# Decay-level products in blocks of 32, and state products of two chunks at once, in a two-layer hybrid trunk

## The chip, the cores and the metric

The kernel runs on one core of a Trainium2 chip. The metric is device time in microseconds (us), from the first to the last instruction with what lies around them; the smaller the better. The engines are PE (TensorE, matmuls), DVE (VectorE), ACT (ScalarE), POOL (GpSimd) and SP (which issues most DMAs). Each runs its own queue in order and waits for others by semaphores.

## The reference, cut to what matters

Two layers work on 512 latent tokens and 128 context tokens of width 1024. In each layer one projection feeds three groups of heads whose outputs meet in one output projection, followed by a feed-forward block. The change touches one of the three, a bidirectional gated recurrence (HGRN2, 6 heads of 64), and the last step that it shares with the retention heads:

```python
def body(S, inp):                       # _hgrn2_chunked, one direction
    qc, bc, kc, vc = inp                # bc: running sum of log forget gates
    inter = jnp.einsum('bhid,bhdv->bhiv', qc * jnp.exp(bc), S)
    rel = bc[:, :, :, None, :] - bc[:, :, None, :, :]
    dec = jnp.exp(jnp.where(tri[:, :, None], rel, -jnp.inf))
    A = jnp.sum(qc[:, :, :, None, :] * kc[:, :, None, :, :] * dec, axis=-1)
    o = inter + jnp.einsum('bhij,bhjv->bhiv', A, vc)
```

It runs once forward and once on the flipped sequence, and the two outputs are added. Retention (`_retention_chunked`) has the same shape with one decay number per head.

## The kernel before

Heads go in pairs: a *channel tile* `ct` (0, 1, 2) holds two heads, head `hh` on partitions 64·hh to 64·hh+63. The 512 latent tokens are four chunks `u` of 128. A fourth call with `ct` None takes the 128 context tokens of all three pairs, as three "chunks".

`hgrn(l, ct)` builds the 128 x 128 matrix A of each chunk and head, both directions at once, transposed (keys on partitions), in the tile `AT`. The decay between key and query depends on the channel, so it cannot be applied after one product. Instead there are eight products: a diagonal one (PSUM tiles `pd`) and one for each of seven *levels* 0 to 6 (`pl`). Level `lev` holds the pairs whose positions lie in the two halves of one aligned block of 2·2^lev tokens. Before each level the queries `Qx` have been multiplied by forget products of the level below (line 855, on DVE), the keys `K` likewise on POOL, and ACT has laid the keys out again as `C` (`composite`). Each product is cut into blocks: in the kernel before, 64 keys by 64 queries, so a chunk and head has two blocks and a call has 4 chunks x 2 heads x 2 blocks = 16 matmuls per product (12 for context). The contraction is over the 64 channels of a head, the result goes to partitions 64·b of the PSUM tile of its head. What a level's 64 x 64 block holds beyond that level is masked off: levels 0 to 4 go into `AT` by a predicated copy on DVE (line 860, mask `msk`), level 5 by eight ACT copies of 32 partitions (line 865), level 6, whose pairs lie in different blocks of 64, by four ACT copies (line 869), after one ACT copy (line 857) has moved the second block's part of `AT` to its place.

`cross_out` makes the output of one `ct` in the PSUM tile `o`. For each chunk: two directions x two heads of state times decayed queries (line 741: 64 channels by 64 outputs by 128 tokens, partitions of head `hh` in and out), then two products with `AT` (line 745: 128 keys). One ACT copy (line 757) takes all four chunks to `raw`. `retention` calls it too. The feed-forward and the projections use matmuls of a type with one pass (`mm3`, lines 220 to 222: three products of high and low parts); all of the above are plain float32.

PE's order is fixed by the program: `Order` steps threads (`hgrn`, `retention`, `fourier` and so on) by a clock of its own, advanced by `o.pe(...)`, and a level is issued 2.4 of those microseconds after the one before it at the earliest, with projection matmuls between. The order on the other engines is made by a list scheduler from its own estimates. PSUM is eight banks handed out in turn.

Names on DVE in the rows below: `jb` is a product-and-sum of the modulation (lines 313 and 315), `wlo` the low part of a weight tile (line 208), `rx` and `rxs` the rotary step of retention, `F`, `PF`, `K`, `PK` the gates.

Of the kernel before, what the change touches and what calls it, by code (L numbers as in the profile page):

```python
# [11 lines left out]
U8 = mybir.dt.uint8  # L12
# [17 lines left out]
def pick(t2, p0, p1, off, dims):  # L30
    b = t2[p0:p1, 0:1]
    return bass.AP(b.tensor, b.offset + off, [list(list(b.ap)[0])] + [list(d) for d in dims])
# [119 lines left out]
class Kernel:  # L152
# [313 lines left out]
    def mixers(self, l, hT, mp):  # L466
        nc, a, o = self.nc, self.a, self.o
# [6 lines left out]
        self.raws, self.mix = [None] * 6, [None] * NK  # L474
        mskf = self.m4("mskf", (128, 7, 128))
        nc.sync.dma_start(mskf, a["masks"])
        self.msk = mp.tile([128, 5, 64], U8, name="msk")
        for b in (slice(0, 64), slice(64, 128)):
            nc.vector.tensor_copy(self.msk[b], mskf[b, 0:5, b])
        self.free(mskf)  # L480
        self.forget_bounds(l)
        self.PF, self.PK = self.m3("PF", (128, 2, 3, 128)), self.m3("PK", (128, 2, 3, 128))
# [246 lines left out]
    def cross_out(self, kind, ct, AT, S, Qd, V):  # L729
        nc = self.nc  # L730
        base = 3 if kind == 0 else 0
        po = self.ps("o")
        nu = 3 if ct is None else 4
        for u in range(nu):
            tt, cc = (4, u) if ct is None else (u, ct)
            out = po[:, u * 128:(u + 1) * 128]
            if ct is not None:
                for d in range(2):
                    for hh in range(2):
                        hs = slice(64 * hh, 64 * hh + 64)  # L740
                        nc.tensor.matmul(out[hs], S[hs, d, u if d == 0 else 3 - u, :], Qd[d][hs, u * 128:(u + 1) * 128],
                                         start=(d == 0), stop=False)
            for hh in range(2):
                v = V[cc][:, tt] if ct is not None or kind else self.prompt_v(cc)[:, 0]
                nc.tensor.matmul(out[64 * hh:64 * hh + 64], v[:, 64 * hh:64 * hh + 64], AT[:, hh, u, :],
                                 start=(ct is None), stop=True)
        self.o.pe(3.2 if ct is not None else 1.0)
        self.free(AT)
        if ct is None:
            for c in range(3):  # L750
                nc.scalar.copy(self.raws[base + c][:, 512:640], po[:, c * 128:(c + 1) * 128])
            self.free(*V)
        else:
            self.free(S)
            self.owed -= kind == 0
            self.raws[base + ct] = self.get("ax", "raw", (128, T))
            nc.scalar.copy(self.raws[base + ct][:, 0:512], po)

    def center(self, out, x, n, heads=2):

# [9 lines left out]
    def hgrn(self, l, ct):  # L770
# [3 lines left out]
        nc = self.nc  # L774
# [4 lines left out]
        if ct is None:  # L779
            bases = (self.PF, self.PK, self.Pq)  # L780
            F, K = (t.rearrange("p d c w -> p d (c w)") for t in (self.PF, self.PK))
            q = self.Pq.rearrange("p c w -> p (c w)")
        else:
            bases = self.hg.pop(ct)
            F, K, q = bases
        nu = 3 if ct is None else 4
        W = nu * 128
        Qx = self.m4("Qx", (128, 2, W))
        ks = self.m2("ks", (128, W))
        nc.gpsimd.tensor_tensor(ks, K[:, 0, :], K[:, 1, :], ALU.add)  # L790
        nc.vector.tensor_tensor(Qx, F, q.unsqueeze(1).to_broadcast([128, 2, W]), ALU.mult)
        AT = self.m4("AT", (128, 2, nu, 128))
        Qf, Kf = Qx.rearrange("p d w -> p (d w)"), K.rearrange("p d w -> p (d w)")
# [5 lines left out]
        def composite(lev):  # L799
            s = 1 << lev  # L800
            C = self.mem.again(Cs.popleft(), "C", (128, W))
            Cs.append(C)
            nc.scalar.copy(pick(C, 0, 128, 0, [[2 * s, W // s // 2], [s, 2], [1, s]]),
                           pick(Kf, 0, 128, 0, [[2 * s, W // s // 2], [W + s, 2], [1, s]]))
            return C

        C = composite(0)
# [2 lines left out]

        A = AT.rearrange("p h u i -> p (h u) i")

        def halves(name):
            return [self.ps(name)[:, 0:W // 2].rearrange("p (u i) -> p u i", u=nu) for _ in range(2)]

        def blocks():
            for u in range(nu):
                for hh in range(2):
                    for b in range(2):
                        t0 = u * 128 + 64 * b  # L820
                        yield slice(64 * hh, 64 * hh + 64), slice(64 * b, 64 * b + 64), hh, u, b, t0

        pd = halves("pd")
        for pr, rows, hh, u, b, t0 in blocks():
            nc.tensor.matmul(pd[hh][rows, u], ks[pr, t0:t0 + 64], q[pr, t0:t0 + 64], start=True, stop=True)
        self.o.pe(0.44 * nu)
        self.free(ks, bases[2])
        for hh in range(2):
            nc.scalar.copy(AT[:, hh, :, 0:64], pd[hh])
        yield 1.0  # L830
        S = None
        for lev in range(7):
            s = 1 << lev
            nb = W // s
            np_ = nb // 2
            pl = halves("pl")
            for pr, rows, hh, u, b, t0 in blocks():
                if lev < 6:
                    qs = pick(Qf, pr.start, pr.stop, t0, [[2 * s, 32 // s], [W + s, 2], [1, s]])
                else:  # L840
                    qs = Qf[pr, (1 - b) * W + t0 + 64 - 128 * b:(1 - b) * W + t0 + 128 - 128 * b]
                nc.tensor.matmul(pl[hh][rows, u], C[pr, t0:t0 + 64], qs, start=True, stop=True)
            self.o.pe(0.44 * nu)

            for d in range(2):
                kv = pick(Kf, 0, 128, d * (W + s), [[2 * s, np_], [1, s]])
                tv = pick(Tt, 0, 128, toff + (nb + 1 if d == 0 else 0), [[2, np_], [0, s]])
                self.kv.tensor_tensor(kv, kv, tv, ALU.mult)
            if lev < 6:
                C = composite(lev + 1)  # L850
            self.kv.tensor_tensor(pick(Tn, 0, 128, tnext, [[np_, 2], [1, np_]]),
                                  pick(Tt, 0, 128, toff, [[nb, 2], [2, np_]]),
                                  pick(Tt, 0, 128, toff + 1, [[nb, 2], [2, np_]]), ALU.mult)
            qv = pick(Qf, 0, 128, 0, [[W + s, 2], [2 * s, np_], [1, s]])
            nc.vector.tensor_tensor(qv, qv, pick(Tt, 0, 128, toff + 1, [[nb - 1, 2], [2, np_], [0, s]]), ALU.mult)
            if lev == 6:
                nc.scalar.copy(A[64:128, :, 64:128], A[64:128, :, 0:64])
            for hh in range(2):
                if lev < 5:
                    nc.vector.copy_predicated(AT[:, hh, :, 0:64], self.msk[:, lev, :].unsqueeze(1).to_broadcast([128, nu, 64]),  # L860
                                              pl[hh])
                elif lev == 5:
                    for b in range(4):
                        rows, cols = slice(32 * b, 32 * b + 32), slice(32 - 32 * (b % 2), 64 - 32 * (b % 2))
                        nc.scalar.copy(AT[rows, hh, :, cols], pl[hh][rows, :, cols])
                else:
                    for b in range(2):
                        rows = slice(64 * b, 64 * b + 64)
                        nc.scalar.copy(AT[rows, hh, :, 64 - 64 * b:128 - 64 * b], pl[hh][rows])
            Tt, toff, tnext = Tn, tnext, tnext + 2 * np_  # L870
            if lev == 0:
                self.free(bases[0])
            if lev == 5:
                self.free(*Cs)
            if lev == 4 and ct is not None:
                yield lambda: self.can(m4=1)
                S = self.new_states(l, 1, ct)
            if lev == 1:
                self.mark(("Hfree", ct))
            yield P["lev"]  # L880
# [4 lines left out]
        for d in range(2):  # L885
            for n in range(3):
                u = n if ct is None or d == 0 else n + 1
# [634 lines left out]
```

## Time and profile before

| | |
|---|---|
| Median of three runs | 1721.58 us (1717.36 to 1722.53) |
| Profiled execution | 1719.44 us |
| its span, first to last instruction | 1717.7 us |
| around the span | 1.7 us |
| PE busy | 1651.0 us, 96% |
| DVE busy | 1056.3 us, 61% |
| ACT busy | 698.5 us, 41% |
| POOL busy | 452.5 us, 26% |

The stage with the changed functions ("mixers") lasts from about 97 to 320 us in layer 0 and from about 940 to 1145 us in layer 1; the rest is projections and feed-forward. Busy time of PE counts overlapping matmuls once.

### The profile page before, as it was taken

To read this page: it belongs to the slowest core of one execution; us is meant where nothing else is said; L and a number is where in the kernel's file an instruction comes from. 1 tells how busy PE (TensorE), PEld (TensorE's weight loads), DVE (VectorE), ACT (ScalarE), POOL (GpSimd) and SP (SyncE) were. 2 spreads that over 40 slices of the span, in tenths; PEclk is the share of its full clock that TensorE was granted. 3 is DMA by queue.
4 is the path that set the end of the run, shared out by engine and by line. 5 is a ranking of instruction groups with operands and counts; after the bars stand their busy time and mean duration, and the time that the engine had idled before them with its cause. 6 is when DMAs were issued, how large, how long until landed. Compare 5 with 4: busy or idle time off the path is not lost. (4 is left out here: it accounts for less than half of the span.)

```text
span 1717.7 us, 31084 instructions
## 1 busy us (share of the span) xinstructions
PE 1651.0 (96%) x12594; PEld 1517.4 (88%) x12594; DVE 1056.3 (61%) x1849; ACT 698.5 (41%) x1368; POOL 452.5 (26%) x474
## 2 busy tenths in 40 slices
PE   6989898999999999999999999999999999999997
PEld 4888787888999998989989988879799999999996
DVE  4788966458668776777493547664754434343428
ACT  4534443826544443434164444485352222121210
POOL 2134532104355453544042334320310000000002
PEclk9999999999999999999999999999999999999999
DMA  9544411243355454544123122024134222121201
GB/s 343 189 136 151 132 52 39 68 176 109 121 194 185 160 181 139 184 135 155 66 102 104 63 77 70 31 72 162 47 114 144 76 73 87 62 92 56 99 25 62
DMA packets 70991, 194.55 MB, mean 113 GB/s; under 512 B 11952, under 2 KB 12736, under 8 KB 70848
## 3 DMA queue, kind: packets, MB, share of 16 engines
q1 hardware_dynamic: 66528, 182.10, 31.7%
q0 software_dynamic: 4032, 10.35, 1.7%
q8 instruction: 99, 1.62, 0.4%
q14 instruction: 44, 0.36, 0.1%
q10 hardware_dynamic: 288, 0.11, 0.0%
HBM read 186.47 MB, written 6.06 MB: 112 GB/s over the span
## 5 line engine op out<-in xcount | busy, mean ns | idle before, releaser
L208 DVE TENSOR_TENSOR wlo<-wraw,whi 128x1024 fp32r<-128x1024 f32 x204 | 268.3, 1316 | 242.9 <-ACT whi L207 237.2
L207 ACT CAST whi<-wraw 128x1024 fp32r<-128x1024 f32 x206 | 214.9, 1048 | 400.0 <-PE pg L221 128.0
L317 POOL TENSOR_TENSOR wm<-wm,csb 128x512 f32<-128x512 f32 x112 | 178.9, 1616 | 184.3 <-DVE jb L313 171.1
L222 PE MATMUL pg<-h2T,wlo 128*128 128x384 f32 (+1 forms) x704 | 218.2, 310 | 3.2 <-DVE wlo L208 3.1
L220 PE MATMUL pg<-h2T,whi 128*128 128x384 f32 (+1 forms) x704 | 218.3, 310 | 0.0
L221 PE MATMUL pg<-h2T,whi 128*128 128x384 f32 (+1 forms) x704 | 217.8, 309 | 0.0
L221 PE MATMUL pu<-h2T,whi 128*128 128x384 f32 (+1 forms) x704 | 217.2, 308 | 0.0
L222 PE MATMUL pu<-h2T,wlo 128*128 128x384 f32 (+1 forms) x704 | 217.2, 308 | 0.0
L220 PE MATMUL pu<-h2T,whi 128*128 128x384 f32 (+1 forms) x704 | 217.2, 308 | 0.0
L341 POOL TENSOR_SCALAR bnve<-bnag 128x1 f32<-128x1 f32 x40 | 13.8, 350 | 657.2 <-DVE bnag L339 652.6
L220 PE MATMUL dps<-whi,ah 128*128 128x512 f32 x440 | 171.6, 390 | 0.0
L222 PE MATMUL dps<-whi,al 128*128 128x512 f32 x440 | 171.5, 390 | 0.0
L221 PE MATMUL dps<-wlo,ah 128*128 128x512 f32 x440 | 171.4, 389 | 0.0
L313 DVE SCALAR_TENSOR_TENSOR jb<-wm,csb 128x512 bf16<-128x512 f32 x160 | 149.0, 931 | 16.7 <-DMA wm<-in_w_modT 10.8
L222 PEld LDWEIGHTS pg<-h2T,wlo 128*128 128x128 f32 x704 | 134.0, 190 | 3.7 <-DVE wlo L208 3.6
L290 ACT ACTIVATE wm<-wm 128x512 f32<-128x512 f32 x112 | 70.8, 632 | 158.5 <-POOL wm L317 158.3
L220 PEld LDWEIGHTS pg<-h2T,whi 128*128 128x128 f32 x704 | 134.2, 191 | 0.3
L221 PEld LDWEIGHTS pg<-h2T,whi 128*128 128x128 f32 x704 | 134.1, 191 | 0.3
L221 PEld LDWEIGHTS pu<-h2T,whi 128*128 128x128 f32 x704 | 133.7, 190 | 0.0
L220 PEld LDWEIGHTS pu<-h2T,whi 128*128 128x128 f32 x704 | 133.7, 190 | 0.0
L222 PEld LDWEIGHTS pu<-h2T,wlo 128*128 128x128 f32 x704 | 133.6, 190 | 0.0
L1216 DVE TENSOR_TENSOR sg<-sg,pu 128x256 f32<-128x256 f32 x88 | 42.7, 485 | 119.6 <-PE pu L222 113.0
(277 smaller groups left out, 3752.9 us busy)
## 6 DMA issues: line engine op xcount, KB each, us to landing
wm<-in_w_modT SPq DMA_DIRECT2D x160, 256.0 KB, 2.9
wraw<-in_w_gate SPq DMA_DIRECT2D x44, 512.0 KB, 3.8
wraw<-in_w_up SPq DMA_DIRECT2D x44, 512.0 KB, 3.4
wraw<-in_w_down SPq DMA_DIRECT2D x44, 512.0 KB, 3.3
wraw<-in_w_fm SPq DMA_DIRECT2D x42, 512.0 KB, 3.3
wm<-in_w_mod SPq DMA_DIRECT2D x16, 512.0 KB, 10.2
wraw<-in_w_tm SPq DMA_DIRECT2D x16, 512.0 KB, 3.4
wraw<-in_w_out SPq DMA_DIRECT2D x16, 512.0 KB, 3.3
```

The costliest lines, as they stand in the source:

```text
L207: self.nc.scalar.copy(hi, raw)
L208: (eng or self.nc.vector).tensor_tensor(lo, raw, hi.bitcast(F32), ALU.subtract)
L220: mm(out, lh, rh, start=first, stop=False)
L221: mm(out, lh, rl, start=False, stop=False)
L222: mm(out, ll, rh, start=False, stop=last)
L290: keep(nc.scalar.activation(out=t, in_=t, func=AF.Copy, accum_out=d))
L313: keep(nc.vector.scalar_tensor_tensor(self.jb, wt, 1.0, csb[0], ALU.mult, ALU.mult, accum_out=d[0]))
L317: nc.gpsimd.tensor_tensor(wt, wt, csb[1], ALU.mult)
L341: nc.gpsimd.tensor_scalar(ve, ag[:, 1:2], EPS, None, ALU.add)
L1216: nc.vector.tensor_tensor(sg, sg, pu[:, :n], ALU.mult)
```

## The change

All products but level 6 are now made of blocks of 32 keys by 32 queries: a chunk and head has four of them, and a product 32 matmuls (24 for context) that go to partitions 32·b. PSUM, the ACT copy of the diagonal, the mask and the predicated copies are half as wide. Level 5 is no longer inside a block: its queries come from the neighbouring block of 32, and its eight ACT copies put it beside the diagonal blocks. The blocks that belong on the diagonal of `AT` are moved there by three ACT copies at level 5 (one copy at level 6 before). `cross_out` has two PSUM tiles and takes two chunks together; the second chunk's heads write to swapped halves of the second tile, so four state products in a row use four different pairs of input and output halves. The second tile leaves PSUM by two ACT copies that cross partitions, the first by one.

```diff
-        self.msk = mp.tile([128, 5, 64], U8, name="msk")
+        self.msk = mp.tile([128, 5, 32], U8, name="msk")
...
-        po = self.ps("o")
...
+        po = [self.ps("o") for _ in range(1 if ct is None else 2)]
+        for a in range(0, 3 if ct is None else 4, len(po)):
+            dst = [(u, hh, po[x][64 * (hh ^ x):64 * (hh ^ x) + 64, (u // len(po)) * 128:(u // len(po)) * 128 + 128])
+                   for x, u in enumerate(range(a, a + len(po))) for hh in range(2)]
             if ct is not None:
                 for d in range(2):
-                    for hh in range(2):
+                    for u, hh, out in dst:
                         hs = slice(64 * hh, 64 * hh + 64)
-                        nc.tensor.matmul(out[hs], S[hs, d, u if d == 0 else 3 - u, :], Qd[d][hs, u * 128:(u + 1) * 128],
+                        nc.tensor.matmul(out, S[hs, d, u if d == 0 else 3 - u, :], Qd[d][hs, u * 128:(u + 1) * 128],
...
-            nc.scalar.copy(self.raws[base + ct][:, 0:512], po)
+            raw = self.raws[base + ct][:, 0:512].rearrange("p (a x i) -> p x a i", a=2, x=2)
+            ov = [p[:, 0:256].rearrange("p (a i) -> p a i", a=2) for p in po]
+            nc.scalar.copy(raw[:, 0], ov[0])
+            for hh in range(2):
+                nc.scalar.copy(raw[64 * hh:64 * hh + 64, 1], ov[1][64 - 64 * hh:128 - 64 * hh])
...
-        pd = halves("pd")
-        for pr, rows, hh, u, b, t0 in blocks():
-            nc.tensor.matmul(pd[hh][rows, u], ks[pr, t0:t0 + 64], q[pr, t0:t0 + 64], start=True, stop=True)
+        pd = parts("pd", 32)
+        for pr, rows, hh, u, b, t0 in blocks(32):
+            nc.tensor.matmul(pd[hh][rows, u], ks[pr, t0:t0 + 32], q[pr, t0:t0 + 32], start=True, stop=True)
...
+            n = max(s, 32)
+            pl = parts("pl", n)
+            for pr, rows, hh, u, b, t0 in blocks(n):
+                if lev < 5:
+                    qs = pick(Qf, pr.start, pr.stop, t0, [[2 * s, 16 // s], [W + s, 2], [1, s]])
                 else:
-                    qs = Qf[pr, (1 - b) * W + t0 + 64 - 128 * b:(1 - b) * W + t0 + 128 - 128 * b]
-                nc.tensor.matmul(pl[hh][rows, u], C[pr, t0:t0 + 64], qs, start=True, stop=True)
+                    i0 = (1 - b % 2) * W + t0 + n - 2 * n * (b % 2)
+                    qs = Qf[pr, i0:i0 + n]
+                nc.tensor.matmul(pl[hh][rows, u], C[pr, t0:t0 + n], qs, start=True, stop=True)
...
-            if lev == 6:
-                nc.scalar.copy(A[64:128, :, 64:128], A[64:128, :, 0:64])
+            if lev == 5:
+                for b in range(1, 4):
+                    rows = slice(32 * b, 32 * b + 32)
+                    nc.scalar.copy(A[rows, :, rows], A[rows, :, 0:32])
...
-                    nc.vector.copy_predicated(AT[:, hh, :, 0:64], self.msk[:, lev, :].unsqueeze(1).to_broadcast([128, nu, 64]),
+                    nc.vector.copy_predicated(AT[:, hh, :, 0:32], self.msk[:, lev, :].unsqueeze(1).to_broadcast([128, nu, 32]),
```

On PE the groups of matmuls stand in the same sequence as before; only their number changes. Here is the end of the first channel tile in layer 0, where `cross_out` is followed by the diagonal product of the second tile, on PE, before:

```order
L741 MATMUL o<-Qx,S 64x128 x4
L745 MATMUL o<-AT,VH_135 64x128 x2
L741 MATMUL o<-Qx,S 64x128 x4
L745 MATMUL o<-AT,VH_135 64x128 x2
L741 MATMUL o<-Qx,S 64x128 x4
L745 MATMUL o<-AT,VH_135 64x128 x2
L741 MATMUL o<-Qx,S 64x128 x4
L745 MATMUL o<-AT,VH_135 64x128 x2
L825 MATMUL pd<-q,ks 64x64 x16
```

and of the changed kernel:

```order
L742 MATMUL o<-Qx,S 64x128 x8
L747 MATMUL o<-AT,VH_135 64x128 x4
L742 MATMUL o<-Qx,S 64x128 x8
L747 MATMUL o<-AT,VH_135 64x128 x4
L829 MATMUL pd<-q,ks 32x32 x32
```

Eight turns between the two kinds of product have become four, and the 16 matmuls of the diagonal 32.

On DVE the scheduler has moved other work. In layer 0, first channel tile, around the query product that ends level 3 (`Qx`, 128x2x32x8), before:

```order
L313 SCALAR_TENSOR_TENSOR jb,acc<-wm,csb 128x512
L208 TENSOR_TENSOR wlo<-wraw,whi 128x1024
L315 SCALAR_TENSOR_TENSOR jb,acc<-wm,csb 128x512
L855 TENSOR_TENSOR Qx<-Qx,Tm 128x2x32x8
L860 COPY_PREDICATED AT<-msk,pl 128x4x64 x2
```

and of the changed kernel, where the query product has line 861 and the predicated copy line 868:

```order
L313 SCALAR_TENSOR_TENSOR jb,acc<-wm,csb 128x512
L315 SCALAR_TENSOR_TENSOR jb,acc<-wm,csb 128x512
L861 TENSOR_TENSOR Qx<-Qx,Tm 128x2x32x8
L868 COPY_PREDICATED AT<-msk,pl 128x4x32 x2
L313 SCALAR_TENSOR_TENSOR jb,acc<-wm,csb 128x512
L208 TENSOR_TENSOR wlo<-wraw,whi 128x1024
```

The low part of a weight tile now stands behind the query product.

The third place is the same engine in layer 1, first channel tile, around the query product that ends level 4 (128x2x16x16), before:

```order
L860 COPY_PREDICATED AT<-msk,pl 128x4x64
L208 TENSOR_TENSOR wlo<-wraw,whi 128x1024
L516 TENSOR_SCALAR F<-F,om,lbv 128x512
L516 TENSOR_SCALAR PF<-PF,om,lbv 128x128
L518 TENSOR_SCALAR K<-K,om 128x512
L518 TENSOR_SCALAR PK<-PK,om 128x128
L855 TENSOR_TENSOR Qx<-Qx,Tm 128x2x16x16
```

and of the changed kernel:

```order
L868 COPY_PREDICATED AT<-msk,pl 128x4x32 x2
L861 TENSOR_TENSOR Qx<-Qx,Tm 128x2x16x16
L517 TENSOR_SCALAR F<-F,om,lbv 128x512
L517 TENSOR_SCALAR PF<-PF,om,lbv 128x128
L519 TENSOR_SCALAR K<-K,om 128x512
L519 TENSOR_SCALAR PK<-PK,om 128x128
```

Here the query product has moved ahead of four gate products and a weight's low part.

## Rows read from the trace of the kernel before

**Rows 1.** The page, busy time, share of the span and instructions of each engine

```profile
PE 1651.0 (96%) x12594; PEld 1517.4 (88%) x12594; DVE 1056.3 (61%) x1849; ACT 698.5 (41%) x1368; POOL 452.5 (26%) x474
```

**Rows 2.** Stretches: length, busy PE, PEld, DVE, ACT, POOL, clock, DMA share, GB/s

```profile
97.00:200.00 103.00, 92.36 (x1101) 85.30 (x1099) 93.79 (x211) 42.67 (x102) 44.24 (x50) 0.98 0.46 150
228.00:320.00 92.00, 83.81 (x987) 71.95 (x980) 52.81 (x110) 44.43 (x103) 24.50 (x31) 0.95 0.16 50
940.00:1145.00 205.00, 198.85 (x2487) 177.58 (x2485) 120.65 (x238) 100.38 (x237) 75.39 (x102) 1.00 0.19 63
```

**Rows 3.** Waits of PE, 97 to 228 us: total, times, longest

```profile
PE pl L842 <- DVE Qx L855: 10.9, 7, 2.8
PE o L741 <- DVE S L717: 1.8, 2, 1.0
```

**Rows 4.** Timeline of PE: start, length, instructions; a diagonal product and a level 0

```profile
98.39 0.69 PE L825 MATMUL pd<-q,ks 64*64 64x64 f32 x32
99.01 0.39 PE L220 MATMUL tps<-whi,hT 128*128 128x256 f32 x1
...
102.08 0.90 PE L842 MATMUL pl<-Qx,C 64*64 64x64 f32 x32
102.91 0.38 PE L220 MATMUL tps<-whi,hT 128*128 128x256 f32 x1
```

**Rows 5.** The same diagonal product, timeline cut at 98.390 and at 98.410 us

```profile
98.39 0.27 PE L825 MATMUL pd<-q,ks 64*64 64x64 f32 x1
98.39 0.29 PE L825 MATMUL pd<-q,ks 64*64 64x64 f32 x4
```

**Rows 6.** Timeline of PE: levels that PE had waited for, layers 0 and 1

```profile
112.55 0.69 PE L842 MATMUL pl<-Qx,C 64*64 64x64 f32 x32 [1.81 <-DVE Qx L855]
...
124.08 0.69 PE L842 MATMUL pl<-Qx,C 64*64 64x64 f32 x32 [2.78 <-DVE Qx L855]
...
227.34 0.89 PE L842 MATMUL pl<-Qx,C 64*64 64x64 f32 x32 [2.43 <-DVE Qx L855]
...
972.66 0.69 PE L842 MATMUL pl<-Qx,C 64*64 64x64 f32 x32 [1.20 <-DVE Qx L855]
```

**Rows 7.** Timeline of PE: a level of the context tokens, and what follows

```profile
1113.44 0.58 PE L842 MATMUL pl<-Qx,C 64*64 64x64 f32 x24
1113.95 0.44 PE L220 MATMUL prq<-hT,whi 128*128 128x384 f32 x1
```

**Rows 8.** Timeline of PE: one cross_out of layer 1, first turn and what follows

```profile
1098.65 0.65 PE L741 MATMUL o<-Qx,S 64*64 64x128 f32 x8
1099.23 0.44 PE L745 MATMUL o<-AT,VH 128*64 128x128 f32 x4
...
1102.46 0.30 PE L842 MATMUL pl<-Qx,C 64*64 64x64 f32 x4
```

**Rows 9.** Timeline of PE: products with 32 and with 64 output partitions

```profile
14.01 0.44 PE L249 MATMUL modps<-wm,cs 128*32 128x128 f32 x4
...
249.82 0.92 PE L701 MATMUL U<-VH,KT 128*64 128x64 f32 x24
```

**Rows 10.** Groups by form: count, busy us, mean ns, idle before

```profile
L860 DVE COPY_PREDICATED AT<-msk,pl 128x256 f32<-128x256 uint8 x60 | 25.2, 441 | 7.4 <-PE pl L842 7.4
L860 DVE COPY_PREDICATED AT<-msk,pl 128x192 f32<-128x192 uint8 x20 | 6.9, 368 | 9.3 <-PE pl L842 9.3
...
L869 ACT COPY AT<-pl 64x256 f32<-64x256 f32 x24 | 8.8, 366 | 0.2
L757 ACT COPY raw<-o 128x512 f32<-128x512 f32 x12 | 7.0, 586 | 22.9 <-PE o L745 22.9
...
L857 ACT COPY AT<-AT 64x512 f32<-64x512 f32 x6 | 3.7, 617 | 0.2
```

**Rows 11.** Timeline of DVE, two weight tiles' low parts in layer 0

```profile
121.09 1.63 DVE L208 TENSOR_TENSOR wlo<-wraw,whi 128x1024 fp32r<-128x1024 f32 x1
...
224.34 1.64 DVE L208 TENSOR_TENSOR wlo<-wraw,whi 128x1024 fp32r<-128x1024 f32 x1
```

More of the change, by code (lines that the diff above doesn't have):

```diff
@@ L476, in mixers @@
         nc.sync.dma_start(mskf, a["masks"])
-        self.msk = mp.tile([128, 5, 64], U8, name="msk")
-        for b in (slice(0, 64), slice(64, 128)):
-            nc.vector.tensor_copy(self.msk[b], mskf[b, 0:5, b])
+        self.msk = mp.tile([128, 5, 32], U8, name="msk")
+        for b in range(4):
+            rows = slice(32 * b, 32 * b + 32)
+            nc.vector.tensor_copy(self.msk[rows], mskf[rows, 0:5, rows])
         self.free(mskf)
@@ L731, in cross_out @@
         base = 3 if kind == 0 else 0
-        po = self.ps("o")
[L733 to L736, printed above, removed]
+        po = [self.ps("o") for _ in range(1 if ct is None else 2)]
+        for a in range(0, 3 if ct is None else 4, len(po)):
+            dst = [(u, hh, po[x][64 * (hh ^ x):64 * (hh ^ x) + 64, (u // len(po)) * 128:(u // len(po)) * 128 + 128])
+                   for x, u in enumerate(range(a, a + len(po))) for hh in range(2)]
             if ct is not None:
                 for d in range(2):
-                    for hh in range(2):
+                    for u, hh, out in dst:
                         hs = slice(64 * hh, 64 * hh + 64)
-                        nc.tensor.matmul(out[hs], S[hs, d, u if d == 0 else 3 - u, :], Qd[d][hs, u * 128:(u + 1) * 128],
+                        nc.tensor.matmul(out, S[hs, d, u if d == 0 else 3 - u, :], Qd[d][hs, u * 128:(u + 1) * 128],
                                          start=(d == 0), stop=False)
-            for hh in range(2):
+            for u, hh, out in dst:
+                tt, cc = (4, u) if ct is None else (u, ct)
                 v = V[cc][:, tt] if ct is not None or kind else self.prompt_v(cc)[:, 0]
-                nc.tensor.matmul(out[64 * hh:64 * hh + 64], v[:, 64 * hh:64 * hh + 64], AT[:, hh, u, :],
-                                 start=(ct is None), stop=True)
+                nc.tensor.matmul(out, v[:, 64 * hh:64 * hh + 64], AT[:, hh, u, :], start=(ct is None), stop=True)
         self.o.pe(3.2 if ct is not None else 1.0)
@@ L750, in cross_out @@
             for c in range(3):
-                nc.scalar.copy(self.raws[base + c][:, 512:640], po[:, c * 128:(c + 1) * 128])
+                nc.scalar.copy(self.raws[base + c][:, 512:640], po[0][:, c * 128:(c + 1) * 128])
             self.free(*V)
@@ L811, in hgrn, with parts, blocks @@
         A = AT.rearrange("p h u i -> p (h u) i")
-        def halves(name):
-            return [self.ps(name)[:, 0:W // 2].rearrange("p (u i) -> p u i", u=nu) for _ in range(2)]
-        def blocks():
+        def parts(name, n):
+            return [self.ps(name)[:, 0:nu * n].rearrange("p (u i) -> p u i", u=nu) for _ in range(2)]
+        def blocks(n):
             for u in range(nu):
                 for hh in range(2):
-                    for b in range(2):
-                        t0 = u * 128 + 64 * b
-                        yield slice(64 * hh, 64 * hh + 64), slice(64 * b, 64 * b + 64), hh, u, b, t0
-        pd = halves("pd")
-        for pr, rows, hh, u, b, t0 in blocks():
-            nc.tensor.matmul(pd[hh][rows, u], ks[pr, t0:t0 + 64], q[pr, t0:t0 + 64], start=True, stop=True)
+                    for b in range(128 // n):
+                        yield slice(64 * hh, 64 * hh + 64), slice(n * b, n * b + n), hh, u, b, u * 128 + n * b
+        pd = parts("pd", 32)
+        for pr, rows, hh, u, b, t0 in blocks(32):
+            nc.tensor.matmul(pd[hh][rows, u], ks[pr, t0:t0 + 32], q[pr, t0:t0 + 32], start=True, stop=True)
         self.o.pe(0.44 * nu)
@@ L828, in hgrn @@
         for hh in range(2):
-            nc.scalar.copy(AT[:, hh, :, 0:64], pd[hh])
+            nc.scalar.copy(AT[:, hh, :, 0:32], pd[hh])
         yield 1.0
@@ L835, in hgrn @@
             np_ = nb // 2
[L836 to L839, printed above, removed]
-                else:
-                    qs = Qf[pr, (1 - b) * W + t0 + 64 - 128 * b:(1 - b) * W + t0 + 128 - 128 * b]
-                nc.tensor.matmul(pl[hh][rows, u], C[pr, t0:t0 + 64], qs, start=True, stop=True)
+            n = max(s, 32)
[3 more added lines that the diff above has]
+                    qs = pick(Qf, pr.start, pr.stop, t0, [[2 * s, 16 // s], [W + s, 2], [1, s]])
+                else:
+                    i0 = (1 - b % 2) * W + t0 + n - 2 * n * (b % 2)
+                    qs = Qf[pr, i0:i0 + n]
+                nc.tensor.matmul(pl[hh][rows, u], C[pr, t0:t0 + n], qs, start=True, stop=True)
             self.o.pe(0.44 * nu)
@@ L855, in hgrn @@
             nc.vector.tensor_tensor(qv, qv, pick(Tt, 0, 128, toff + 1, [[nb - 1, 2], [2, np_], [0, s]]), ALU.mult)
-            if lev == 6:
-                nc.scalar.copy(A[64:128, :, 64:128], A[64:128, :, 0:64])
+            if lev == 5:
+                for b in range(1, 4):
+                    rows = slice(32 * b, 32 * b + 32)
+                    nc.scalar.copy(A[rows, :, rows], A[rows, :, 0:32])
             for hh in range(2):
                 if lev < 5:
-                    nc.vector.copy_predicated(AT[:, hh, :, 0:64], self.msk[:, lev, :].unsqueeze(1).to_broadcast([128, nu, 64]),
+                    nc.vector.copy_predicated(AT[:, hh, :, 0:32], self.msk[:, lev, :].unsqueeze(1).to_broadcast([128, nu, 32]),
                                               pl[hh])
[L862 to L865, printed above, removed]
-                else:
-                    for b in range(2):
-                        rows = slice(64 * b, 64 * b + 64)
-                        nc.scalar.copy(AT[rows, hh, :, 64 - 64 * b:128 - 64 * b], pl[hh][rows])
+                else:
+                    for b in range(128 // n):
+                        rows, cols = (slice(n * i, n * i + n) for i in (b, b ^ 1))
+                        nc.scalar.copy(AT[rows, hh, :, cols], pl[hh][rows])
             Tt, toff, tnext = Tn, tnext, tnext + 2 * np_
```

## The prediction

> **What bounds the kernel now.** I read the page first: PE is busy for 96% of the span, DVE for 61%, ACT for 41% [rows 1]. So the kernel is bound by PE, and PE time saved is kept wherever PE does not wait. The table by stretches shows where that is so. In layer 1's mixers PE is busy for 198.85 of 205.00 us, and in layer 0 from 228 to 320 us for 83.81 of 92.00. But from 97 to 200 us DVE has 93.79 of 103.00 and PE 92.36: there DVE, which also works on the modulation, sets the pace [rows 2]. The list of waits agrees: from 97 to 228 us PE waits 10.9 us in seven pieces for `Qx`, the query product on DVE, before a level, and 1.8 us for states [rows 3]. What PE saves in this stretch mostly lengthens such waits; what DVE saves ahead of `Qx` shortens them.
>
> Then I read single groups in the timeline. A diagonal product of 64-blocks has 32 records for its 16 matmuls, so a float32 matmul leaves two, each a load and a product. From its start to that of the next projection matmul it takes 0.62 us; level 0, whose queries are read in the finest interleaving, 0.83 us [rows 4]; a context product 0.51 us [rows 7]. Taken from first to last start (a row's length less one matmul, 0.22 us) they are 0.47, 0.68 and 0.36 us. The rest, 0.15 us, is paid at the turn to another kind of matmul and stays.
>
> **The change, part by part.**
>
> *Products by 32.* Matmuls double: 64 records in place of 32, each with half the columns, on eight pieces of the array. Two prices are in question. One is how long a piece is held: eight steps of 0.47/8 = 0.059 us now, at half the columns about 0.029. The other is how closely records can start. Cut at 98.390 us the timeline has one matmul of the group, cut at 98.410 it has four, and the row grows from 0.27 to 0.29 us: three gaps in 20 ns, some 6.5 ns each [rows 5]. Eight pieces need 8 x 6.5 = 52 ns for a step, more than 29, so the start of records decides: 64 x 6.5 = 0.42 us from first to last. That PE can be fed so fast is not shown for 64 records; what is shown is that a group which it had waited 1.81 us for ran through its 32 at the usual 0.69 us [rows 6]. That four pieces of 32 output columns work side by side is shown, by a row of four that lasts 0.44 us [rows 9]; eight are not.
>
> Bounds: below, if only the piece's time counts, 0.29 us per product (7 x 0.029 and the first step's lag), 4.5 ns per record. Above, today's average, 0.47/32 = 14.7 ns per record, thus 0.94 us. I take 6.5 ns, the row of the same operation nearest to it. Then a product saves 0.47 - 0.42 = 0.05 to 0.06 us, level 0 0.27 (its slow reading is halved too and disappears below 52 ns), a context product 0.36 - 0.31 = 0.05. A channel tile has seven such products (diagonal, levels 0 to 5): 6 x 0.06 + 0.27 = 0.63 us; context 7 x 0.05 = 0.35. Layer 1: 3 x 0.63 + 0.35 = **2.2 us**. In layer 0 after 228 us one product and the context's: **0.4 us**.
>
> The Trainium skill says otherwise (TensorE: Matmul & The Clock Gate, section "Wait — 56ns, not 53.3ns?"): starts of matmuls are never closer than about 25 ns, however few columns they have. The trace has four starts in 21 ns [rows 5], so the rule does not hold between different pieces of the array; held by it, the 2080 records of layer 1 and of layer 0 after 228 us would take 52 us where I count 13.5, and the sum would be about 1735.
>
> *State products.* A `cross_out` takes 1102.46 - 1098.65 = 3.81 us: four times eight records of state products (0.58 us to the next kind) and four of the other (0.37) [rows 8]. Two of four pieces work at a time; swapping the second chunk's heads fills all four, so 16 records take the 0.58 us of eight, plus 0.01 for starts. The products with `AT` contract over 128 keys and still have two pieces: eight records take 0.37 and another two steps, 0.21 (0.65 - 0.44, the difference of eight and four in a row), so 0.58. Together 2 x (0.59 + 0.58) = 2.34 us; 1.45 saved, and four turns with it. Twelve calls have it: six in layer 1, **8.7 us**; four in layer 0 after 228 us, **5.8 us**. Two fall before and I count nothing for them, since the next `Qx` sets the pace.
>
> *DVE.* A predicated copy takes 441 ns at 256 elements and 368 at 192 [rows 10], 73 ns per 64, so at 128 about 295: 0.146 us less, ten times per call. With that the order moves. Before level 4 of the first tile PE waited 2.78 us [rows 6] behind a `wlo` of 1.63 us [rows 11] which now stands behind `Qx`; six narrower copies are 0.9 more. Together 2.5 of the 2.78. The projection that follows is the second half of an older weight tile's, so this `wlo` may be late. At 227.34 us it is the same: `wlo` of 1.64 and a shuffle move behind `Qx`, and the wait of 2.43 us [rows 6] should go, 2.4. In the second tile the order gives as much as it takes: one more `jb` ahead of `Qx` against the narrower copies; nothing. So **4.9 us**. In layer 1 `Qx` moves ahead of four gate products and a `wlo`: the wait of 1.20 us at 972.66 goes [rows 6], **1.2 us**. Bounds: nothing, if what is moved is wanted at once elsewhere, and the 6.1.
>
> *ACT.* One copy of `raw` (586 ns) becomes one of 128 x 256 and two of 64 x 256 (366 ns each for such a copy out of PSUM), near 1.1 us; one copy inside `AT` (617 ns) becomes three of 32 partitions, at most 366 each [rows 10]. A call gains about 1.0 us of ACT work. I cost it at nothing: ACT is busy for 100.38 of 205.00 us in layer 1 [rows 2], `raw` is wanted only when all heads are done, and the three copies come one product earlier than the one did. Without that cover the last `raw` of a layer delays the head norms by 0.5 us, 1.0 in all. The three copies wait for the predicated copies of level 4 in ACT's queue, and a weight's cast or the next `C` stands behind them; that is where a loss would begin. A second PSUM tile per `cross_out` hastens the turn of the eight banks; what PE waits for most is results of DVE, not banks [rows 3], so nothing.
>
> *Sum*, against the profiled execution: 1719.4 - 2.2 - 0.4 - 8.7 - 5.8 - 4.9 - 1.2 = **1696 us**. That execution lies 2.1 us under the median of the runs, within their range.
>
> **Rivals.**
>
> *Pieces do not limit each other at the start of records*: 4.5 ns in place of 6.5 takes 2080 x 2.0 = 4 us more: 1692. For it: starts of 6.5 ns may be all that the engine was asked for. Against: the gap is the same in all steps of the group.
>
> *PE saves, but the moved work on DVE and the added work on ACT are wanted at once*: no 6.1 us, and 1.0 to 2 us lost on ACT: 1704. For it: DVE has 93.79 of 103.00 us, so what moves behind `Qx` delays something.
>
> *Records come at today's average*, 14.7 ns: 2080 x 14.7 = 30.6 us in place of the present 16.0, so 1719.4 + 14.6 - 14.5 - 6.1 = 1713.
>
> *Slower: PE's supply of small matmuls is the bound.* The 24 records of a state update, on two pieces, take (0.92 - 0.27)/24 = 27 ns each [rows 9]. At this price the 2080 records take 56 us, 40 more than now, and the 20 products between 97 and 228 us grow by 1.26 us each, 25, of which the waits of 12.7 [rows 3] hide half: 1719.4 + 40 - 14.5 - 6.1 + 12 = 1751. It decides from (16.0 + 14.5 + 6.1)/2080 = 17.6 ns on. For it: no group in the rows has more than 32 such records, so a longer run is not shown. Against: the 14.7 ns of a group that came right after a wait [rows 6]. The rule of the Trainium skill above (TensorE: Matmul & The Clock Gate, the same section) is of this kind; no run here shows it for pieces side by side.
>
> *The change does not do what it says*: eight pieces run as two fours. Sixteen steps of 0.029, 0.47 us, leave a plain product where it is: 1699, inside the forecast's range.
>
> **How the numbers follow.** The forecast (with the last case) 0.64; closer starts 0.08; DVE and ACT take their part back 0.14; today's average 0.07; slower 0.07. The likeliest is 1696, of its own 1690 to 1704. The range from 1689 to 1712 leaves out the average's and the slower case's ends, 0.14, and some 0.04 below. A measurement of this kernel tells apart about 0.3%, 5.2 us: faster is all up to about 1716, 0.87; within 0.06, slower 0.07.
>
> **What would show it.** The diagonal product and a plain level: 64 records in one row of about 0.64 us in place of 0.69; four starts again within 21 ns, and eight within 46. A `cross_out` of 2.3 to 2.4 us in place of 3.81, with four turns. Predicated copies near 295 ns. Waits for `Qx` near 0.3 at the first tile's level 4, none at 227 and 972 us. PE busy down by about 20 us. It would be wrong if a 64-record row is near 1 us or longer, if PE waits for `wlo` or `whi` where it did not before, or if state products with swapped heads still run in steps of two.

## The result, and the profile after

The changed kernel takes 1711.35 us (median of 6 runs, 1708.78 to 1714.33), the kernel before 1721.34 beside it (1717.36 to 1722.72): ratio 0.9944, 95% interval 0.9933 to 0.9956. It is faster by 10 us; the forecast of 1696 had 25. The profiled executions took 1719.44 and 1708.78 us, 10.7 apart, so 12.7 of the 23.4 us from 1719.4 down to 1696 are missing.

Section 1 of the page of the changed kernel, then its table of stretches (columns as in [rows 2]):

```profile
PE 1638.5 (96%) x14274; PEld 1515.1 (89%) x14274; DVE 1046.6 (61%) x1853; ACT 707.1 (41%) x1408; POOL 459.2 (27%) x474
```

```profile
97.00:200.00 103.00, 94.62 (x1647) 87.50 (x1645) 93.64 (x223) 46.91 (x115) 45.18 (x54) 0.98 0.49 153
228.00:320.00 92.00, 80.03 (x1130) 70.90 (x1130) 56.34 (x111) 53.02 (x123) 21.44 (x27) 0.94 0.18 53
940.00:1145.00 205.00, 196.36 (x3293) 180.10 (x3282) 121.41 (x244) 112.15 (x263) 71.55 (x92) 0.98 0.20 61
```

PE's busy time fell by 12.5 us, not by 20 [rows 1]. In layer 1 PE is idle for 8.64 of 205 us where it was for 6.15, and its granted clock fell from 1.00 to 0.98 [rows 2]. PE's timeline shows the two parts of the change alone, a diagonal product and a cross_out of layer 1:

```profile
97.94 0.76 PE L829 MATMUL pd<-q,ks 64*32 64x32 f32 x64
98.62 0.39 PE L220 MATMUL tps<-whi,hT 128*128 128x256 f32 x1
...
1089.25 0.67 PE L742 MATMUL o<-Qx,S 64*64 64x128 f32 x16
1089.84 0.66 PE L747 MATMUL o<-AT,VH 128*64 128x128 f32 x8
1090.43 0.67 PE L742 MATMUL o<-Qx,S 64*64 64x128 f32 x16
1091.03 0.66 PE L747 MATMUL o<-AT,VH 128*64 128x128 f32 x8
1091.62 0.65 PE L848 MATMUL pl<-Qx,C 64*32 64x32 f32 x48
```

The cross_out takes 1091.62 - 1089.25 = 2.37 us in place of 3.81 [rows 8], as forecast. A product by 32 takes 98.62 - 97.94 = 0.68 us up to the next kind, 0.06 more than by 64 [rows 4], not 0.06 less.

Where the time went shows in PE's waits. The first two rows are those of the kernel before, which the prediction did not look at: 228 to 320 us, then 940 to 1145 (total, times, longest).

```profile
PE pr L928 <- DVE rx L542: 7.1, 3, 4.6
...
PE pr L928 <- DVE rx L542: 2.9, 2, 1.9
```

The same two rows of the changed kernel:

```profile
PE pr L932 <- DVE rx L543: 9.1, 3, 4.6
...
PE pr L932 <- DVE rx L543: 5.7, 2, 3.1
```

`pr`, the first product of a retention, waits for `rx`, the rotated queries and keys, and does so 4.8 us longer in all. Three waits grew, from 1.37, 1.91 and 1.00 to 3.30, 3.13 and 2.53 us. PE's timeline of the kernel before at these three:

```profile
265.14 1.16 PE L928 MATMUL pr<-rx 64*128 64x128 f32 x16 [1.37 <-DVE rx L542]
...
1075.29 1.16 PE L928 MATMUL pr<-rx 64*128 64x128 f32 x16 [1.91 <-DVE rx L542]
...
1124.07 1.16 PE L928 MATMUL pr<-rx 64*128 64x128 f32 x16 [1.00 <-DVE rx L542]
```

and of the changed kernel:

```profile
257.76 1.81 PE L932 MATMUL pr<-rx 64*128 64x128 f32 x16 [3.30 <-DVE rx L543]
259.51 1.11 PE L935 MATMUL pk<-ident,rx 128*128 128x128 f32 x4
...
1064.36 2.08 PE L932 MATMUL pr<-rx 64*128 64x128 f32 x16 [3.13 <-DVE rx L543]
1066.37 1.11 PE L935 MATMUL pk<-ident,rx 128*128 128x128 f32 x4
...
1109.20 0.67 PE L742 MATMUL o<-Qr,S 64*64 64x128 f32 x16
1109.80 0.66 PE L747 MATMUL o<-AT,VR 128*64 128x128 f32 x8
1110.39 0.62 PE L848 MATMUL pl<-Qx,C 64*32 64x32 f32 x48
1113.54 1.16 PE L932 MATMUL pr<-rx 64*128 64x128 f32 x16 [2.53 <-DVE rx L543]
```

The last of them reads most plainly: a cross_out and a level stand ahead of `pr`, while ACT copies the projection out and DVE rotates it in four operations. `rx` is ready when these are done, whatever PE does; the 1.44 us that this cross_out saves are 1.53 us more of waiting. In the first place a cross_out stands ahead of `pr` too. In the second it is in part DVE's order, in its timeline:

```profile
1059.41 0.74 DVE L540 STREAM_SHUFFLE rxs<-rx 128x512 f32<-128x512 f32 x1
1060.04 0.28 DVE L868 COPY_PREDICATED AT<-msk,pl 128x128 f32<-128x128 uint8 x1
1060.23 0.85 DVE L541 TENSOR_TENSOR rx<-rx,rope 128x512 f32<-128x512 f32 x1
1061.01 0.68 DVE L542 TENSOR_TENSOR rxs<-rxs,rope 128x512 f32<-128x512 f32 x1
1061.61 2.01 DVE L208 TENSOR_TENSOR wlo<-wraw,whi 128x1024 fp32r<-128x1024 f32 x1
1063.54 0.68 DVE L543 TENSOR_TENSOR rx<-rx,rxs 128x512 f32<-128x512 f32 x1
```

A `wlo` of 2.01 us now stands ahead of the rotary's last sum; before, the `wlo` of this place ran ahead of the shuffle. From the shuffle's start to that of `pr` it is 4.95 us now and was 4.42. The other 0.7 us of the longer wait is PE's being earlier here against DVE: the level ahead of `pr` starts 1.07 us behind the shuffle, where it was 1.81.

Behind each of these waits PE also runs slower. The table of stretches, 5 us each, of the changed kernel (the granted clock is the number behind POOL's):

```profile
255.00:260.00 5.00, 2.24 (x19) 2.02 (x20) 4.03 (x9) 0.39 (x1) 1.70 (x2) 0.81 0.32 111
260.00:265.00 5.00, 5.00 (x94) 4.82 (x94) 3.28 (x8) 2.12 (x6) 0.00 (x0) 0.85 0.01 3
1060.00:1065.00 5.00, 1.87 (x75) 1.66 (x75) 4.82 (x7) 3.52 (x12) 1.72 (x2) 0.86 0.09 12
1065.00:1070.00 5.00, 5.00 (x27) 4.78 (x26) 1.29 (x2) 1.35 (x4) 0.00 (x0) 0.50 0.26 96
1115.00:1120.00 5.00, 5.00 (x117) 4.21 (x119) 3.13 (x10) 4.70 (x18) 0.00 (x0) 0.67 0.10 36
```

and of the kernel before, behind its `pr` at 265.14 and 1075.29 us:

```profile
265.00:270.00 5.00, 4.86 (x61) 4.64 (x65) 4.19 (x10) 1.55 (x5) 0.90 (x2) 1.00 0.04 10
1075.00:1080.00 5.00, 4.71 (x38) 4.62 (x39) 2.37 (x5) 3.25 (x10) 0.00 (x0) 1.00 0.00 0
```

0.50 is the lower of the clock's two levels, 1.2 of 2.4 GHz; PE had waited 3.13 us before it fell. From the start of `pr` to where the rows have their usual length again, the changed kernel loses against the kernel before 1.5 us at the first place, 2.8 at the second and 0.9 at the third: 5.2.

That is one execution of each kernel, but the mean granted clock of every run agrees: on average 0.988 over the six runs of the changed kernel, 0.992 over 48 of the kernel before. The profiled pair, 0.988 and 0.993, lies a little wider apart than that, so 5.2 is rather too much for the usual run.

### The profile page after: what moved, and what is told of

It is laid out like the page before. It is cut to its first block, busy times and chain, and to the rows that moved or that the text cites. A ratio compares the mean times of both kernels' runs of the same rounds, so it can differ in the third digit from the quotient of the medians.

```text
span 1707.0 us, 34478 instructions
## 1 busy us (share of the span) xinstructions
PE 1638.5 (96%) x14274; PEld 1515.1 (89%) x14274; DVE 1046.6 (61%) x1853; ACT 707.1 (41%) x1408; POOL 459.2 (27%) x474
## 4 chain that ended last, share of the span: by engine, by line
PE 81%; DVE 9%; ACT 4%; issue 2%; POOL 2%; DMA 2%; DVEq 0%; SPq 0%; POOLq 0%; ACTq 0%
PE pg L222 6%; PE pu L220 6%; PE pu L222 6%; PE pu L221 6%; PE pg L221 6%; PE pg L220 6%; PE dps L222 6%; PE dps L221 6%; PE dps L220 6%; PE p L220 2%; PE ops L222 2%; PE ops L220 2%; PE ops L221 2%; PE p L221 2%; PE tps L220 2%
```

## The experiments

**Theory A**: cross_out's saving is real, but where PE next waits for the rotary it becomes waiting, and the longer wait brings a stretch at the lower clock. **Theory B**: the products by 32 take what is missing.

**pairs_only**: the kernel before with the change's part in cross_out alone (the pieces of the diff from `po` to `raw`). 

> State products for two chunks at once, diagonal and level products by 64 as before, so PE's order is that of the kernel before. Theory A (the gain was given back at the rotary steps: `pr` waits for `rx` on DVE longer by what PE saved ahead of it, and TensorE's clock is at its lower level after such a wait): the wait at the second retention of layer 0 grows from 1.37 to near 3 us, that at the last of layer 1 from 1.00 to near 2.5, and of the 14.5 us that ten cross_out save some 6 are lost there: 1712 to 1715. Theory B (what is missing is the price of the products by 32): cross_out keeps its 14.5 us: near 1707.

**blocks_only**: the rest of the diff, without those pieces. 

> Products up to the sixth level by 32, state products as before. The prediction's own terms: 2.6 for the products and 6.1 for DVE's order: near 1712.6. Theory A: the products cost about 0.06 us more each instead of less (1.5 us over layer 1 and the end of layer 0), DVE's order gives some 5 in layer 0; at the first retention of layer 1 a wlo stands between the rotary's operations and costs 1 to 4: 1717 to 1721. Theory B, in which all of the missing 12.7 us is the products': 1721 to 1726.

Measured: pairs_only 1716.8 (ratio 0.9976, 0.9966 to 0.9986), blocks_only 1715.9 (0.9975, 0.9965 to 0.9985), beside 1720.15 before. Neither is what B says. Ten calls that save 14.5 us of PE gave 4: less still than A's 1712 to 1715, with the waits that A named, PE's timeline of pairs_only in layer 0:

```profile
262.52 2.08 PE L932 MATMUL pr<-rx 64*128 64x128 f32 x16 [3.35 <-DVE rx L542]
264.53 1.11 PE L935 MATMUL pk<-ident,rx 128*128 128x128 f32 x4
```

In layer 1's last retention the wait is 2.78 us. The new cross_out alone thus makes two of the three waits longer. In layer 1's first retention pairs_only waits 1.91 us, as the kernel before does; yet `pr` took 2.01 us there, at the lower clock, where it took 1.09 before. So a longer wait is not the whole condition for a slow stretch.

blocks_only gained more than A expected; its waits at the three places are 1.35, 2.38 and 0.77 us and `pr` runs at 1.09 us in all of them. Behind the wait of 2.38 us the clock falls one group later (0.82 from 1075 to 1080 us), and some 1.6 us are lost. Over all runs the granted clock is 0.988 in the twelve of pairs_only and 0.991 in the eleven of blocks_only: most of the changed kernel's loss of clock comes with the new cross_out.

**warm**: PE is kept at work in the waits.

```diff
+        pk = self.ps("pk")
+        for _ in range({(0, 1): 20, (0, 2): 30, (1, 0): 20, (1, 2): 14}.get((l, ct), 0)):
+            nc.tensor.transpose(pk[:, 0:128], self.ident, self.ident)
...
-        pk = self.ps("pk")
```

> The changed kernel with 20, 30, 20 and 14 transposes of the identity (0.109 us each) into pk's bank ahead of `pr` in four retentions that wait for `rx`; pk overwrites them. They fill 2.2, 3.3, 2.2 and 1.5 us of the waits of 3.30, 4.57, 3.13 and 2.53 us, and delay nothing. Theory A: the clock stays at its higher level behind them, the rows of `pr` take 1.09 instead of 1.74 to 2.01 us, and 4 to 6 us come back: 1705.5 to 1707.5. If the lower clock there has another cause, or the waits are all that costs: 1711 to 1712.

Measured: 1705.2 us (0.9909, 0.9894 to 0.9924), 6 less than the changed kernel, for transposes that compute nothing. At the second place, its timeline:

```profile
1063.02 2.41 PE L931 MATMUL pk<-ident 128*128 128x128 f32 x20
1066.00 1.16 PE L935 MATMUL pr<-rx 64*128 64x128 f32 x16 [0.57 <-DVE rx L543]
1067.09 0.66 PE L937 MATMUL pk<-ident,rx 128*128 128x128 f32 x4
```

`pk` takes 0.66 in place of 1.11 us, and the granted clock from 1065 to 1070 us is 1.00. Over its five runs the mean clock is 0.993.

**warm_before**: the same 30 transposes in the kernel before, ahead of layer 0's third retention. 

> The kernel before with 30 transposes of the identity ahead of `pr` in layer 0's third retention, where it waits 4.62 us for `rx`, the one long wait that both kernels have. What warm gave (6.2 us) is then split: Theory A: here 1.5 to 2.5 us come back, 1719 of 1721.3, and the other 4 us of warm belong to the waits that the change made longer. If filling this one wait gives 5 or more (1716), the clock's loss was there before the change and explains nothing of its missing gain.

 Measured: 1719.5 beside 1719.3 (1.000, 0.9991 to 1.001). `pr` there ran in 1.09 us, and the rows of the two profiles gain 1.9 us at this place, but by the medians the time did not move, with some 1.6 us each way: less than expected. So most of warm's 6 us can't have come from this wait, which both kernels have. By the rows of warm beside the changed kernel's it gave 1.7 us of them, and the three that the change made longer 1.5, 2.8 and 0.3. Such rows are of one execution, and here the runs gave less than they suggest.

**later_ret** and **before_later**: the planner starts a retention later, with one number changed in the changed kernel and in the kernel before.

```diff
-P = dict(... r=6.5, b=6.5, ...)
+P = dict(... r=11.0, b=6.5, ...)
```

> The changed kernel with the planner told that a retention may start 11.0 us after its last projection by its own count, in place of 6.5: at the second retention of layer 0 and the first of layer 1 a projection (and a level) come in ahead of `pr`. Theory A: the waits of 3.30 and 3.13 us there shrink below 1, and with them the clock's loss: 4 to 7 us faster than the changed kernel, 1704 to 1707. Against: the retentions end later, and the waits at the end of the mixers grow by as much: 1711 or more.

> The kernel before with the same one number (6.5 to 11.0) as in later_ret. Theory A: what the later start gives depends on the waits that the change made longer; before it, the two places wait 1.37 and 1.91 us and `pr` runs at 1.09, and the third retention of layer 0 waits 4.62: 4 to 9 us faster than before, 1712 to 1716, so that the change itself is worth 16 to 20 us on top of it. If the later start is worth the 15 us of later_ret by itself, whatever the change: 1705.

Measured: later_ret 1696.1 (0.9859, 0.9844 to 0.9873), before_later 1710.2 (0.9936, 0.9920 to 0.9952). The first retention of layer 1 in later_ret:

```profile
1058.42 0.69 PE L848 MATMUL pl<-Qx,C 64*64 64x64 f32 x32
1059.04 1.16 PE L932 MATMUL pr<-rx 64*128 64x128 f32 x16
1060.13 0.66 PE L935 MATMUL pk<-ident,rx 128*128 128x128 f32 x4
```

No wait is left there. The 15 us are far more than the 4 to 7 that A gave for it, and part of the reason is that the later start gives the kernel before 11 us as well, more than expected: waiting for `rx` was already dear. What belongs to the change is the difference: with the later start it is worth 14 us (1710.2 to 1696.1) in place of 10, less than A's 16 to 20. By the ratios it is 13.3 with some 4 each way beside 9.6 with 2, so that it is worth more with the later start is likely and not beyond the noise.

**pairs_later**: the new cross_out alone, with 11.0. 

> State products for two chunks at once with products by 64, and the later start (11.0). Theory A with products by 32 dearer by 0.06 us but narrower copies and another order of DVE in layer 0: the order of DVE was worth 5 to 6 us by the traces of pairs_only and the changed kernel up to 228 us, the products cost 1.5: 1699 to 1702. If the products by 32 are a loss on the whole: below 1696.

 Measured: 1703.7 (0.9898, 0.9879 to 0.9916). The products by 32, with the narrower copies and DVE's order that come with them, are worth 7.6 us on top (to 1696.1; by the ratios 6.7 with some 4 each way): no loss on the whole. A's 1699 to 1702 was 2 us too low.

**later12**: 12.0 in place of 11.0. 

> The changed kernel with 12.0 in place of 11.0: in layer 1 the last retention's `pr` stands behind one more level of the context. Theory A: its wait of 2.53 us falls to about 1.9 and the clock's loss behind it (some 1 us) goes, 1 to 2 us less than later_ret's 1696.1: 1694 to 1695.5. Against: the level is short (0.43 us) and the end of the mixers is bound by the head norms' chain: 1696 as in later_ret.

 Measured: 1696.7 (0.9860, 0.9839 to 0.9881): the wait for `rx` is gone, but PE waits just as long one group earlier, 3.31 us for `Qx` ahead of the level that now stands in front of `pr`. `pr` takes 2.01 us, at the lower clock, and the time is that of later_ret. A miss.

**later_warm**: later_ret, and transposes in its two waits over 2 us.

```diff
+        for _ in range(14 if (l, kind, ct) == (0, 1, None) else 0):
+            nc.tensor.transpose(pu[:, 0:128], self.ident, self.ident)
...
+        for _ in range({(1, 2): 14}.get((l, ct), 0)):
+            nc.tensor.transpose(pk[:, 0:128], self.ident, self.ident)
```

> later_ret, and transposes of the identity in its two last waits over 2 us: 14 ahead of `pr` of layer 1's last retention (wait 2.53 us) and 14 ahead of the states' products of layer 0's context (wait 2.32 us, for a copy of KT on ACT). Theory A: no stretch at the lower clock is left behind them, 2 to 4 us: 1692.5 to 1694.5. Without an effect of the clock: 1696.

 Measured: 1692.5 (1691.9 to 1695.2; 0.9844, 0.9831 to 0.9858), the fastest kernel of this study. Beside later_ret that is 3.6 us by the medians, and by the ratios 2.6 with some 3.5 each way: as expected, but within the noise.

**act_twice**: the three copies inside AT are made twice.

```diff
                 for b in range(1, 4):
                     rows = slice(32 * b, 32 * b + 32)
                     nc.scalar.copy(A[rows, :, rows], A[rows, :, 0:32])
+                    nc.scalar.copy(A[rows, :, rows], A[rows, :, 0:32])
```

> The changed kernel with its three copies inside AT made twice: eight times 1.2 us more on ACT at the place where the prediction saw the beginning of a loss. Theory A, in which ACT's added work is covered almost everywhere and the rotary chain on DVE is what PE waits for: 1711 to 1714. If ACT's added work is what took the gain: each extra 1.2 us delays a product, 8 to 10 us slower, 1719 or more.

 Measured: 1712.9 (0.9965, 0.9953 to 0.9978). By the medians 1.5 us slower than the changed kernel, by the ratios 3.6 with some 3 each way, for 9.6 us more of ACT: it is covered for the most part.

**price**: four forms of the 64-record group.

```diff
+            for i in (0, 16):
+                nc.tensor.matmul(pd[hh][rows, u, i:i + 16], ks[pr, t0:t0 + 32], q[pr, t0 + i:t0 + i + 16], start=True, stop=True)
...
-            pl = parts("pl", n)
...
+            pl = parts("pl", 64 if lev == 4 else n)
+            turn = list(blocks(n))
+            if lev == 1:
+                turn = turn + turn
+            if lev == 2:
+                turn.sort(key=lambda x: x[4] // 2)
...
+                if lev == 4 and t0 < W - 32:
+                    nc.tensor.matmul(pl[hh][rows, u], C[pr, t0:t0 + 32], pick(Qf, ...), start=True, stop=True)
+                    continue
...
```

> The changed kernel with four other forms of the 64-record group, each in its place: the diagonal product in two matmuls of 16 columns for each of 32 (128 records), level 1 issued twice (128 records), level 2 in turns over four pieces of the array in place of eight (64 records), level 4 with 64 columns (64 records; the second 32 columns, and in the last block nothing, are not used, so level 4's numbers change only in PSUM). Now first to last 0.563 us. If a piece is held in proportion to columns: diagonal 0.56, level 1 1.13, level 2 0.56 or more, level 4 near 1.1. If a piece is held some 65 ns by each record whatever its columns: diagonal 1.13, level 1 1.13, level 2 1.0 to 1.1, level 4 0.56. If the start of records is what limits, 8.8 ns each: diagonal and level 1 1.13, level 2 and level 4 0.56.

Measured in one execution, PE's timeline (level 4's group is cut into many rows by its last block, and only its first stands here):

```profile
998.23 1.41 PE L830 MATMUL pd<-q,ks 64*32 64x16 f32 x128
999.57 0.39 PE L220 MATMUL fo<-ph,c64r 128*128 128x256 f32 x1
...
1007.10 1.29 PE L857 MATMUL pl<-Qx,C 64*32 64x32 f32 x128
1008.32 0.39 PE L220 MATMUL tps<-whi,hT 128*128 128x256 f32 x1
...
1011.38 0.76 PE L857 MATMUL pl<-Qx,C 64*32 64x32 f32 x64
1012.07 0.39 PE L220 MATMUL tps<-whi,hT 128*128 128x256 f32 x1
...
1018.89 0.72 PE L855 MATMUL pl<-Qx,C 64*32 64x64 f32 x50
...
1019.66 0.45 PE L220 MATMUL p<-hT,whi 128*128 128x384 f32 x1
```

Up to the next kind: 1.34 us for twice the records with half the columns, 1.22 for twice the records, 0.69 on four pieces in turn, 0.77 with twice the columns, beside 0.68. The granted clock of this stretch is 1.00. The columns change this time little and the number of pieces not at all; the number of records sets it, (1.22 - 0.68)/64 = 8.4 ns each. Each record has a weight load of its own in all four forms, so whether the start of the load or of the product limits is not told apart.

## Why the prediction was wrong

**The step that failed** is the one that took ten cross_out calls into the sum in full, 8.7 and 5.8 us, because PE is busy for 198.85 of 205 us [rows 2]. Each call is shorter by 1.44 us, where 1.45 was worked out. But a share of busy time does not say what stands behind each call. In two of the three places the next thing is a wait for `rx`, set by ACT and DVE. I listed PE's waits only from 97 to 228 us [rows 3]; the same list for the two stretches in which I counted would have shown 10.0 us for `rx`. That 1711.35 still lies inside the range, 1689 to 1712, is luck: the forecast's own case was to end at 1704, and no rival put waits at the rotary.

**The missing 12.7 us**, by rows of the two profiles: waits for `rx` 4.8 longer (14.8 against 10.0); the lower clock behind them 5.2; the products 3.9 (next paragraph). That is 13.9, 1.2 more than is missing. That much more than the sum's terms came elsewhere: PE's first row stood 0.66 us earlier already, and two cross_out calls were counted at nothing. That the new cross_out makes the waits longer is shown by pairs_only beside blocks_only, and the clock's part by filling the waits (warm). later_ret shows what waiting for `rx` costs in all, not this sum's 4.8. The clock's size is less sure than its sign: warm gave 6 us with an interval of some 3 each way. And not all is recovered: with the later start the change is worth 14 us. Other waits take the place, in layer 0 one of 2.32 us for ACT's copy of the transposed keys `KT`, which stands behind a weight's cast and the three copies of `raw`; and the last one for `rx` stays at 2.53. How much of the remaining 9 us each of them holds was not measured.

**The price of a record** was mis-sized: 6.5 ns from four starts; 8.8 is measured (the row of 0.76 less one matmul of 0.20, by 64), 8.4 in price. A plain product costs 0.06 us more than by 64, where 0.06 less was forecast, and level 1 0.03 more; level 0 gains 0.11, not 0.27. A tile is 5 x 0.06 + 0.03 - 0.11 = 0.22 dearer, a context 7 x 0.045 = 0.3; with three tiles, two contexts and one product more, 1.3 us on, where 2.6 off were counted. That the start of records decides, and not how long a piece is held, was right, as price shows. The rival of today's average, 1713, comes near the measured time by chance: its 14.7 ns are not there. The rule of the Trainium skill (TensorE: Matmul & The Clock Gate, section "Wait — 56ns, not 53.3ns?") that starts are no closer than about 25 ns does not hold here between pieces of the array, even for a run of 128 records, which start 8.6 to 9.6 ns apart ((1.29 - 0.20)/127 and (1.41 - 0.19)/127).

**DVE's order** was right in place and near in size: the wait at the first tile's level 4 is 0.42 us (0.3 forecast), those at 227 and 972 us are gone, predicated copies take 294 ns (295). Against pairs_only, which has the old order, the changed kernel is 0.70 us ahead at PE's first row and 6.15 ahead at the projection at 226.65 us: 5.5 where 4.9 was forecast, some 1.2 of it because pairs_only runs at the lower clock behind its wait of 2.42 us. But the next level, at 230.94 us, now waits 1.14 us for `Qx`, which it did not before, and 4.2 are left there. What I did not ask was where the moved `wlo` would stand next: in layer 1, in the midst of the rotary.

**ACT** costed at nothing held for the most part (act_twice), though a copy inside `AT` takes 403 ns and not at most 366. One wait for ACT is new, 1.31 us for the last copy of `raw` ahead of a level at 203.75 us, in the stretch where the two cross_out calls were counted at nothing. The rival in which DVE and ACT take their part back named the right kind of loss, priced it at 1 to 2 us beside the 6.1, and sought it on ACT at level 4; it was on DVE, at the rotary.

## What to carry to other kernels

Before a saving on the bounding engine is counted, find the next wait behind each place, in each stretch that is counted: if another engine's chain ends there, the saving becomes waiting, and the work must be put in another order (here one number of the planner) before it shows. Longer waits of PE are paid twice when its clock falls behind them, so PE's waits and the granted clock of the stretch behind belong in the same reading. A price taken from the first few starts of a group is a bound, not the price of a long run.

## What the runs showed of the hardware

Small float32 matmuls on pieces of 64 by 32 start 8.4 to 9.6 ns apart in runs of 64 and 128 records, almost whatever the columns (16, 32 or 64) and on four pieces as on eight. On four pieces of 64 by 64 with 64 columns, in the kernel before, it is 14.7 ns [rows 4]. The lower clock does not follow from a wait's length alone: behind `pr`'s wait of 1.24 us in layer 0 the changed kernel's rows keep their usual 1.09 us, in warm the same group behind 1.23 us took 2.01. Behind the same 1.91 us the kernel before took 1.09 us and pairs_only 2.01. What else decides stays open.
